# Whole-row activation loads, zero matmuls in idle gaps, output stores ahead of the branch, a fourth split-weight pair and a fourteenth expert buffer in a hybrid RG-LRU, Conformer and expert trunk

## The chip, the cores and the metric

The kernel runs on one core of a Trainium2 chip. The metric is the device time of one execution in microseconds (us). Three runs of the kernel before gave 1893.31, 1895.31 and 1895.43 us; the median is 1895.31 us.

## What is computed

Two layers of a diffusion trunk over 256 latent tokens and 256 context tokens, 1024 channels wide, in float32. Both streams share the weights.

```python
for i in range(DEPTH):                       # DEPTH = 2
    mod = split(silu(c) @ mod_w[i] + mod_b[i], 6)           # shifts, scales, gates; also from c_ctx
    h = modulate(rmsnorm(x, norm1_g[i]), mod[0], mod[1])
    # mixer: one input projection, two branches, merged by gates
    u_rnn, g_rnn, u_glu, g_glu, g_mrg = split(h @ w_in[i])
    hf, hb = rglru_bidir(u_rnn, ...)         # conv of width 4, gates, one scan per direction
    y_a = ((hf + hb) * gelu(g_rnn)) @ w_a
    y_b = silu(layernorm(dwconv31(u_glu * sigmoid(g_glu)))) @ w_b
    x = x + mod[2] * ((g_a * y_a + g_b * y_b) @ w_out)
    h = modulate(rmsnorm(x, norm2_g[i]), mod[3], mod[4])
    # layer 0: SwiGLU of width 2816; layer 1: top 2 of 8 SwiGLU experts of width 2816
    x = x + mod[5] * ffn(h)
return rmsnorm(x, final_g)                   # the 256 latent tokens alone
```

The latent scans start from the final state of the context scans. In layer 1 the context is only needed for that state.

## The kernel before

**Layout and precision.** Channels lie on the 128 partitions, in 8 blocks (index k), tokens along the row. `X[k]` holds a block's context tokens (`xc`, 256 columns) and latent tokens (`xs`, 256 columns). A float32 weight or activation is split into a high and a low half by `split` and `hilo`: ScalarE rounds the high half (`wh`, `nh`, line 153), VectorE subtracts it from the whole for the low half (`wl`, `nl`, line 154). A product is then three matmuls: high by high, low by high, high by low (lines 273 to 275; in the first projection lines 418 to 420).

**Weights.** Two streams, both issued by SyncE. The dense one, `raw`, comes in chunks of 2 MB with two buffers; a chunk is four pieces of 128x1024, and a piece is one block of 128 output channels of a projection, with 24 matmuls on a split piece. The split pieces live in the pool `hl`, with three pairs `wh`, `wl` before the change. The expert stream, `mraw`, comes in 264 transfers of 1 MB, in two rings of 9 and 4 buffers (`RINGA`, `RINGB`).

**Start.** SyncE issues the small vector constants, `sc` (from which silu(c) is made), the first modulation chunk `m0`, and x in eight transfers of 256 KB. TensorE multiplies the modulation (`pmod`, line 369, and its transposition `pmt`, line 379), then sums squares over channels (`colsum`: `pcol`, line 284; `rstd_cols`: `pst`, line 308, a square root on ScalarE and a reciprocal on VectorE), and spreads the result over the partitions (`spread`: `dg`, line 320, `prs`, line 322). `norm` makes `nt`, `nh` and `nl` from it, and the projection `pu` begins.

**Order of work.** A tile scheduler places the instructions of all engines by priorities and dependencies, so a larger pool moves instructions on engines that the diff does not name. In the mixers TensorE works through the projection while VectorE does convolutions (`cv`), the blocks of recurrent scans (lines 546 to 558) and the low halves `wl`, all in one queue.

**Experts.** `route` and `route_sort` choose two experts per token (`sel`, `pos`, the one-hot `oh`), sort the experts by load, and gather their tokens (`pgat`, `xe`). Every expert is 11 chunks. A chunk is an up projection (`up_big`, lines 1191 to 1193, eight blocks by three matmuls), a swish (`hd`, line 1212), a transposition of the result (`turn_big`: `pht`, line 1219, then the split `hh`, `hlo`) and a down projection (`down_big`, lines 1250 to 1252). The loop in `experts` is staggered: the up projection of chunk n+1 stands ahead of the down projection of chunk n, and `pht` of chunk n right behind its own up projection. Four experts of the eight take up to 128 tokens each ("big"), four take up to 64 ("small"); big and small alternate.

**End.** After the last expert the squares of the latent tokens are summed again, `rsf` is taken, and then every engine branches on whether some expert had too many tokens (line 1111). The body behind the branch repeats the experts for the rest and does not run with these inputs. Behind it stand `spread`, eight multiplications of 128x256 on VectorE (line 1119) and eight stores of 128 KB (line 1120).

Of the kernel before, what the change touches and what calls it, by code (L numbers as in the profile page):

```python
# [6 lines left out]
F32 = mybir.dt.float32  # L7
# [34 lines left out]
RINGA, RINGB, XB = 9, 4, 1  # L42
# [89 lines left out]
class Trunk:  # L132
    def __init__(self, ctx, tc, wd, wm, wv, sr, xt, vec, out, dbg=None, stop=None):
        self.tc, self.nc = tc, tc.nc
        self.wv, self.sr = wv, sr
        self.wd, self.wm, self.xt_d, self.vec_d, self.out = wd, wm, xt, vec, out
        self.dbg, self.stop = dbg or {}, stop
        self.ci = DEPTH
        self.ahead = 100
        self.last_act = None  # L140
        self.gate = None
# [137 lines left out]
    def colsum(self, get, n, tag):  # L279
        nc = self.nc  # L280
        ps = self.ps("pcol")
        for k in range(KD):
            g = k % 4
            nc.tensor.matmul(ps[32 * g:32 * g + 32, 0:n], self.v("om", 0, 32), get(k), start=(k < 4), stop=(k >= 4),
                             tile_position=(0, 32 * g))
        ev = self.t2(tag, "cev")
        nc.scalar.copy(ev[:, 0:n], ps[:, 0:n])
        return ev
# [13 lines left out]

    def rstd_cols(self, ev, n, rs=None):
# [3 lines left out]
        for t in range(nt):  # L307
            nc.tensor.matmul(pt[:, 2 * t:2 * t + 2], ev[:, t * P:(t + 1) * P], self.v("s32", 0, 2), start=True,
                             stop=True)
# [6 lines left out]
    def spread(self, rs, n, tag):  # L316
        nc = self.nc
        dg = self.t2(tag, "dg")
        for t in range(n // P):
            nc.vector.tensor_scalar(dg[:, t * P:(t + 1) * P], self.v("id", 0, P), rs[:, t:t + 1], None, op0=ALU.mult)  # L320
        r = self.ps("prs")
        nc.tensor.matmul(r[:, 0:n], self.v("o1", 0, P), dg[:, 0:n], start=True, stop=True)  # L322
# [35 lines left out]
    def mod_chunk(self, i, q, pool=None, got=None):  # L358
# [7 lines left out]
        for kk in range(2):  # L366
            for g in range(4):
                k = 2 * g + kk
                nc.tensor.matmul(ps[32 * g:32 * g + 32, :], self.sc[:, k, 6 - 2 * r:38 - 2 * r], w[:, k, :],
                                 start=(r == 0 and kk == 0), stop=(end and kk == 1), tile_position=(0, 32 * g))  # L370
# [7 lines left out]
        for t in range(4):  # L378
            nc.tensor.matmul(pt[:, n * t:n * t + n], ev[:, t * P:(t + 1) * P], self.v("sel", 0, n), start=True,
                             stop=True)  # L380
# [22 lines left out]
    def begin(self, X, hx, m0):  # L403
# [409 lines left out]
    def run(self, ctx):  # L813
# [17 lines left out]
        self.hl = left.enter_context(tc.tile_pool(name="hl", bufs=3))  # L831
# [6 lines left out]
        self.start = start.__enter__()  # L838
        m0 = self.chunk(("mod", 0, 0), self.start)
# [138 lines left out]
    def route_end(self):  # L978
# [3 lines left out]
        rs = self.rstd_cols(ev, TC)  # L982
        rt_t = lambda nm, shape: mp.tile(shape, F32, tag=nm, name=nm)
# [24 lines left out]
        nc.tensor.matmul(pv[:, 1, :], tri, sel[:, 1, :], start=False, stop=True)  # L1008
# [87 lines left out]
    def moe(self, X):  # L1096
# [6 lines left out]
        rs = self.mp.tile([P, 4], F32, tag="rsf", name="rsf")  # L1103
# [202 lines left out]
    def experts(self, X, xe):  # L1306
# [4 lines left out]
        for n in range(len(steps) + 2):  # L1311
# [36 lines left out]
            prev = (*new[:2], (self.turn_big if new[0] < BIG else self.turn_small)(new[2])) if new else None  # L1348
# [110 lines left out]
```

## Time and profile before

| | us |
|---|---|
| median of three runs | 1895.31 |
| the profiled execution | 1895.52 |
| its span on the core | 1893.6 |
| TensorE matmuls busy (PE) | 1835.2 |
| VectorE busy (DVE) | 1299.9 |
| ScalarE busy (ACT) | 893.7 |
| data moved | 449.64 MB, mean 237 GB/s |

The span is what the trace covers; the profiled execution took 1.9 us more than it. PE is TensorE's matmuls, PEld its weight loads, DVE VectorE, ACT ScalarE, POOL GpSimd, SP SyncE; a q behind a name is the engine's instruction queue. A row of the timeline gives the start, the duration, the engine, the source line, the operation, what it writes and reads, how many alike follow one another, and in brackets how long the engine stood idle before it and what it waited for.

### The profile page before, as it was taken

What the parts mean: (1) busy time and instruction counts of PE and PEld (TensorE: products, weight loads), DVE (VectorE), ACT (ScalarE), POOL (GpSimd) and SP (SyncE); (2) the same over time, 40 slices, a digit from 0 to 9 for tenths busy, and PEclk for the clock granted to TensorE, in tenths of its full rate; (3) what the DMA queues carried; (4) which work ended last, traced back from release to release, by engine and by line L of the source; (5) the groups of instructions that cost most, each with busy time, mean ns of one, the idle gap of its engine ahead of it and who ended that gap; (6) DMA issues with size and microseconds to landing.
All of it is one profiled execution on the core that took longest, in us unless ns stands there. A gap on an engine that the chain in (4) does not pass through costs nothing. (4 is left out here: it accounts for less than half of the span.)

```text
span 1893.6 us, 26822 instructions
## 1 busy us (share of the span) xinstructions
PE 1835.2 (97%) x10292; PEld 1421.2 (75%) x10292; DVE 1299.9 (69%) x2296; ACT 893.7 (47%) x1266; POOL 0.4 (0%) x5
## 2 busy tenths in 40 slices
PE   6999999999999999999998999999999999999997
PEld 3666777778998888888787998787577568667853
DVE  3899996255679967656999565885298249518922
ACT  4695332253552222225797554674176137416711
POOL 0000000000000000000000000000000000000000
PEclk9999999999999999999999999899999999999998
DMA  8233444222335565421243447689999999999994
GB/s 346 106 112 139 178 178 178 89 89 89 112 116 200 182 225 190 156 89 46 106 151 134 166 180 308 256 339 376 419 420 405 396 420 420 383 413 420 415 386 166
DMA packets 66951, 449.64 MB, mean 237 GB/s; under 512 B 7424, under 2 KB 8576, under 8 KB 24704
## 3 DMA queue, kind: packets, MB, share of 16 engines
q1 hardware_dynamic: 66816, 447.85, 60.5%
q8 instruction: 83, 1.36, 0.3%
q14 instruction: 52, 0.43, 0.1%
HBM read 446.78 MB, written 1.05 MB: 236 GB/s over the span
## 5 line engine op out<-in xcount | busy, mean ns | idle before, releaser
L153 ACT ACTIVATE wh<-raw 128x1024 fp32r<-128x1024 f32 (+1 forms) x237 | 247.3, 1053 | 500.5 <-PE ps L274 317.0
L154 DVE TENSOR_TENSOR wl<-raw,wh 128x1024 fp32r<-128x1024 f32 (+1 forms) x237 | 286.6, 1218 | 137.7 <-ACT wh L153 134.4
L154 DVE TENSOR_TENSOR wl<-mraw,wh 128x1024 fp32r<-128x1024 f32 x264 | 314.6, 1222 | 35.8 <-ACT wh L153 29.2
L153 ACT ACTIVATE wh<-mraw 128x1024 fp32r<-128x1024 f32 x264 | 272.8, 1057 | 51.6 <-PE s L1192 37.6
L273 PE MATMUL ps<-nh,wh 128*128 128x512 f32 (+1 forms) x736 | 273.1, 371 | 1.0 <-ACT wh L153 1.0
L275 PE MATMUL ps<-nh,wl 128*128 128x512 f32 (+1 forms) x736 | 269.5, 366 | 3.1 <-DVE wl L154 3.1
L274 PE MATMUL ps<-nl,wh 128*128 128x512 f32 (+1 forms) x736 | 269.2, 366 | 0.0
L273 PEld LDWEIGHTS ps<-nh,wh 128*128 128x128 f32 x736 | 139.2, 189 | 31.1 <-ACT gab L256 1.7
L1203 PE MATMUL s<-mraw,xes 128*64 128x256 f32 x1408 | 161.9, 380 | 0.0
L275 PEld LDWEIGHTS ps<-nh,wl 128*128 128x128 f32 x736 | 139.0, 189 | 27.7 <-DVE wl L154 3.3
L274 PEld LDWEIGHTS ps<-nl,wh 128*128 128x128 f32 x736 | 139.1, 189 | 25.3 <-issue 1.4
L1193 PE MATMUL s<-wl,xe 128*128 128x512 f32 x352 | 140.6, 399 | 4.2 <-DVE wl L154 4.2
L256 ACT ACTIVATE hd<-s 128x256 f32<-128x256 f32 (+1 forms) x88 | 28.9, 329 | 242.6 <-PE s L1203 218.6
L1191 PE MATMUL s<-wh,xe 128*128 128x512 f32 x352 | 143.0, 406 | 0.0
L1192 PE MATMUL s<-wh,xe 128*128 128x512 f32 x352 | 138.8, 394 | 0.0
L1203 PEld LDWEIGHTS s<-mraw,xes 128*64 128x64 f32 x1408 | 98.2, 137 | 45.0 <-issue 0.7
L1212 DVE TENSOR_TENSOR hd<-hd,s 128x256 f32<-128x256 f32 (+1 forms) x88 | 31.0, 352 | 129.9 <-ACT hd L256 129.8
L572 DVE SCALAR_TENSOR_TENSOR cv<-v,vec,cv 128x254 f32<-128x254 f32 (+14 forms) x240 | 103.6, 481 | 0.8
L232 DVE SCALAR_TENSOR_TENSOR junk<-wv,scr 128x512 f32<-128x512 f32 x128 | 84.1, 687 | 0.2
L1193 PEld LDWEIGHTS s<-wl,xe 128*128 128x128 f32 x352 | 66.9, 190 | 23.0 <-DVE wl L154 8.9
L1258 PE MATMUL y<-mraw,hs 128*64 128x512 f32 x352 | 83.4, 594 | 0.4 <-DVE hs L1237 0.4
L1191 PEld LDWEIGHTS s<-wh,xe 128*128 128x128 f32 x352 | 67.2, 191 | 13.4 <-ACT wh L153 0.7
(283 smaller groups left out, 3540.2 us busy)
## 6 DMA issues: line engine op xcount, KB each, us to landing
mraw<-in_wm_dram SPq DMA_DIRECT2D x264, 1024.0 KB, 9.5
raw<-in_wd_dram SPq DMA_DIRECT2D x65, 2048.0 KB, 7.4
wv<-in_wv_dram SPq DMA_DIRECT2D x96, 256.0 KB, 3.6
lw<-in_wd_dram SPq DMA_DIRECT2D x16, 256.0 KB, 2.9
xc<-in_xt_dram SPq DMA_DIRECT2D x4, 256.0 KB, 10.2
xs<-in_xt_dram SPq DMA_DIRECT2D x4, 256.0 KB, 10.3
scr<-in_sr_dram SPq DMA_DIRECT2D x4, 256.0 KB, 4.9
out_dram<-xs SPq DMA_DIRECT2D x8, 128.0 KB, 2.0
```

The costliest lines, as they stand in the source:

```text
L153: return (self.nc.scalar.activation(hi, src, AF.Copy), self.nc.vector.tensor_tensor(lo, src, hi.bitcast(F32), op=ALU.subtract))
L154: self.nc.vector.tensor_tensor(lo, src, hi.bitcast(F32), op=ALU.subtract))
L232: nc.vector.scalar_tensor_tensor(junk, w[h], 1.0, rows[2 * s + h], op0=ALU.mult, op1=ALU.mult, accum_out=acc[:, h, s:s + 1])
L273: self.nc.tensor.matmul(o, wh, ah, start=(k == 0), stop=False)
L274: self.nc.tensor.matmul(o, wh, al, start=False, stop=False)
L275: self.nc.tensor.matmul(o, wl, ah, start=False, stop=(k == KD - 1))
L572: nc.vector.scalar_tensor_tensor(cv[:, a0:a1], v[:, a0 + d:a1 + d], w(t), cv[:, a0:a1], op0=ALU.mult, op1=ALU.add)
L1191: nc.tensor.matmul(p1, xe[0][:, k, :], wh[:, cs], start=(k == 0), stop=False)
L1192: nc.tensor.matmul(p1, xe[1][:, k, :], wh[:, cs], start=False, stop=False)
L1193: nc.tensor.matmul(p1, xe[0][:, k, :], wl[:, cs], start=False, stop=(k == KD - 1))
L1203: nc.tensor.matmul(p1[r, 0:2 * P].rearrange("p (g f) -> p g f", g=2), xe[:, k, :], w[:, :, h * P:(h + 1) * P], start=(k == 0), stop=(k == ...
L1258: ins = self.nc.tensor.matmul(py[0][r, :], hs[:, f * HALF:(f + 1) * HALF], raw[:, f * PIECE + q * 512:f * PIECE + (q + 1) * 512], start=(c ...
```

## The change

1. **Start.** x comes in two transfers of 1 MB, `xs` second in SyncE's order and `xc` fourth, ahead of `m0`. The squares are shared between ScalarE and VectorE (`square2`). The sums of squares and `spread` stand ahead of the first modulation, which now follows `prs`. The first weight chunk comes in two halves. `dg` is one instruction in place of one per 128 columns. The square root's table is loaded early.
2. **Zero matmuls.** `warm(n)` issues n matmuls on a zero tile whose result nobody reads, ordered behind the last real matmul: 3 of 512 columns ahead of `pcol`, single ones and a pair of 256 columns between the steps of the start, 6 behind `pst` and 4 behind `ppos` in the routing.
3. **Pools.** `hl` has four pairs in place of three; `RINGB` is 5 in place of 4; the DMA scratch of the program is 1 KB.
4. **Experts.** The transposition of the first chunk (n = 0) is put off until after the up projection of the second.
5. **End.** The scale by the final norm's weight (`fg`), `spread`, four multiplications of 128x512 and four stores of 256 KB stand ahead of the branch, and again in its body. Behind the branch nothing is left.

```diff
-RINGA, RINGB, XB = 9, 4, 1
+RINGA, RINGB, XB = 9, 5, 1
...
+    def warm(self, n, cols=TC):
+        ps = self.ps("pwarm")
+        for _ in range(n):
+            ins = self.nc.tensor.matmul(ps[:, 0:cols], self.wz[:, 0:P], self.wz[:, 0:cols], start=True, stop=True).ins
+            if self.last_pe is not None:
+                self.order(ins, self.last_pe)
...
+    def square2(self, tiles):
+        def get(k):
+            sq = self.t2("g", "sq")
+            for s in range(2):
+                x, o = tiles[k][s], sq[:, s * TC:(s + 1) * TC]
+                if (k + s) % 2:
+                    self.nc.vector.tensor_tensor(o, x, x, op=ALU.mult)
+                else:
+                    self.nc.scalar.activation(o, x, AF.Square)
+            return sq
...
-        for t in range(n // P):
-            nc.vector.tensor_scalar(dg[:, t * P:(t + 1) * P], self.v("id", 0, P), rs[:, t:t + 1], None, op0=ALU.mult)
+        nt = n // P
+        nc.vector.tensor_tensor(dg[:, 0:n].rearrange("p (t m) -> p t m", t=nt),
+                                self.v("id", 0, P).unsqueeze(1).to_broadcast([P, nt, P]),
+                                rs[:, 0:nt].unsqueeze(2).to_broadcast([P, nt, P]), op=ALU.mult)
...
-        for _ in self.mod_chunk(0, 0, got=m0):
-            pass
-        ev = self.colsum(self.square(X, 0, T, "g"), T, "g")
-        r = self.spread(self.rstd_cols(ev, T), T, "g")
-        raw = self.chunk(tuple(what))
+        self.warm(3, 512)
+        ev = self.colsum(self.square2(X), T, "g")
+        self.warm(1)
+        rs = self.rstd_cols(ev, T)
+        self.warm(1)
+        r = self.spread(rs, T, "g")
+        m = self.mod_chunk(0, 0, got=m0)
+        next(m)
+        self.warm(1)
+        next(m, None)
+        self.warm(2)
+        self.last_pe, self.wz = None, self.vec[:, VO["id"]:VO["id"] + 512]
+        raw = self.chunk(tuple(what), parts=2)
...
+        nc.sync.dma_start(self.sc, self.vec_d[:, NV:NV + KD * SCW].rearrange("p (k m) -> p k m", m=SCW))
+        nc.sync.dma_start(xs, self.xt_d[1])
         nc.sync.dma_start(self.vec[:, 0:NV0], self.vec_d[:, 0:NV0])
...
+        nc.sync.dma_start(xc, self.xt_d[0])
         m0 = self.chunk(("mod", 0, 0), self.start)
-        for k in range(0, KD, 2):
-            for s, t in enumerate((xc, xs)):
-                nc.sync.dma_start(t[:, k:k + 2, :], self.xt_d[s, :, k:k + 2, :])
...
-        self.hl = left.enter_context(tc.tile_pool(name="hl", bufs=3))
+        self.hl = left.enter_context(tc.tile_pool(name="hl", bufs=4))
...
         rs = self.rstd_cols(ev, TC)
+        self.warm(6)
...
+        self.last_pe = nc.tensor.matmul(pv[:, 1, :], tri, sel[:, 1, :], start=False, stop=True).ins.name
+        self.warm(4)
...
             self.experts(X, xe)
-            self.rstd_cols(self.colsum(self.square(X, TC, T, "rt"), TC, "rt"), TC, rs)
+            rs = self.rstd_cols(self.colsum(self.square(X, TC, T, "rt"), TC, "rt"), TC)
+            o = [self.mp.tile([P, 4, TC], F32, tag=nm, name="o") for nm in ("yl", "yh")]
+            for k in range(KD):
+                nc.vector.tensor_scalar(o[k // 4][:, k % 4], X[k][1], self.v("fg", k), None, op0=ALU.mult)
+            r = self.spread(rs, TC, "rt")
+            for k in range(0, KD, 2):
+                t = o[k // 4][:, k % 4:k % 4 + 2]
+                nc.vector.tensor_tensor(t, t, r[:, 0:TC].unsqueeze(1).to_broadcast([P, 2, TC]), op=ALU.mult)
+                nc.sync.dma_start(self.out[:, k:k + 2, :], t)
...
-        r = self.spread(rs, TC, "rt")
-        for k in range(KD):
-            nc.vector.scalar_tensor_tensor(X[k][1], X[k][1], self.v("fg", k), r[:, 0:TC], op0=ALU.mult, op1=ALU.mult)
-            nc.sync.dma_start(self.out[:, k, :], X[k][1])
...
+                if n == 1:
+                    ph = self.turn_big(ph)
                 big = pe < BIG
...
+            prev = new if n == 0 else (*new[:2], (self.turn_big if new[0] < BIG else self.turn_small)(new[2])) if new else None
...
+    nc = _bacc.Bacc("TRN2", target_bir_lowering=False, num_devices=1, dynamic_dma_scratch_size=1024)
```

In the changed file the lines of the expert loop stand 38 further down (1191 becomes 1229), those of the scans 32 further (546 becomes 578). Three places of the order are shown.

TensorE's first instructions, before the change: the modulation first, then the sums of squares and the projection.

```order
L369 MATMUL pmod<-raw,sc 32x512 x8
L379 MATMUL pmt<-vec,ev 128x2 x4
L284 MATMUL pcol<-sq,vec 32x512 x8
L308 MATMUL pst<-vec,cev 128x2 x4
L322 MATMUL prs<-dg,vec 128x512
L418 MATMUL pu<-nh,wh 128x512
```

The same place after the change (`pwarm` are the zero matmuls):

```order
L272 MATMUL pwarm<-wz 128x512 x3
L292 MATMUL pcol<-sq,vec 32x512 x8
L272 MATMUL pwarm<-wz 128x256
L329 MATMUL pst<-vec,cev 128x2 x4
L272 MATMUL pwarm<-wz 128x256
L345 MATMUL prs<-dg,vec 128x512
L392 MATMUL pmod<-raw,sc 32x512 x8
L272 MATMUL pwarm<-wz 128x256
L403 MATMUL pmt<-vec,ev 128x2 x4
L272 MATMUL pwarm<-wz 128x256 x2
L442 MATMUL pu<-nh,wh 128x512
```

The modulation went from the head to behind `prs`, and every gap between dependent steps holds zero matmuls.

VectorE in the first layer's mixer, before the change, in one of the blocks of scans (`gi`, `r`, `hs` are its tiles; the listing gives a scan the name of its family, the trace calls it a scan; `wl` is the low half of a weight piece, `v` the gated input of the Conformer branch):

```order
L552 SCALAR_TENSOR_TENSOR r<-a,r,gi 128x256
L548 SCALAR_TENSOR_TENSOR r<-a,gi 128x512
L546 TENSOR_TENSOR gi<-gi,e_1254 128x512
L558 TENSOR_TENSOR hs<-r 128x512
L550 SCALAR_TENSOR_TENSOR r<-a,gi 128x256
L154 TENSOR_TENSOR wl<-raw,wh 128x1024
L552 SCALAR_TENSOR_TENSOR r<-a,r,gi 128x256
L154 TENSOR_TENSOR wl<-raw,wh 128x1024
L558 TENSOR_TENSOR hs<-r 128x512
```

The same block after the change, from its fourth operation:

```order
L582 SCALAR_TENSOR_TENSOR r<-a,gi 128x256
L578 TENSOR_TENSOR gi<-gi,e_1257 128x512
L584 SCALAR_TENSOR_TENSOR r<-a,r,gi 128x256
L580 SCALAR_TENSOR_TENSOR r<-a,gi 128x512
L578 TENSOR_TENSOR gi<-gi,e_1263 128x512
L590 TENSOR_TENSOR hs<-r 128x512
L582 SCALAR_TENSOR_TENSOR r<-a,gi 128x256
L155 TENSOR_TENSOR wl<-raw,wh 128x1024
L584 SCALAR_TENSOR_TENSOR r<-a,r,gi 128x256
L688 SCALAR_TENSOR_TENSOR v<-v,pglu 128x512
L590 TENSOR_TENSOR hs<-r 128x512
```

The first of the two `wl` has left the block and stands ten rows ahead of its first scan operation; the second stands where the first stood.

TensorE at the first experts' chunks, before the change (`s_10522` is the up projection of chunk 0, `s_10573` that of chunk 1):

```order
L1191 MATMUL s_10522<-wh,xe_10422 128x512
L1192 MATMUL s_10522<-wh,xe_10423 128x512
L1193 MATMUL s_10522<-wl,xe_10422 128x512
L1219 MATMUL pht<-vec,hd 128x128 x2
L1191 MATMUL s_10573<-wh,xe_10422 128x512
L1192 MATMUL s_10573<-wh,xe_10423 128x512
```

After the change (`s_10578` is the up projection of chunk 1, `y` the down projection of chunk 0):

```order
L1229 MATMUL s_10578<-wh,xe_10435 128x512
L1230 MATMUL s_10578<-wh,xe_10436 128x512
L1257 MATMUL pht<-vec,hd 128x128 x2
L1231 MATMUL s_10578<-wl,xe_10435 128x512
L1229 MATMUL s_10578<-wh,xe_10435 128x512
L1230 MATMUL s_10578<-wh,xe_10436 128x512
L1231 MATMUL s_10578<-wl,xe_10435 128x512
L1288 MATMUL y<-wh,hh 128x512
```

The transposition of chunk 0 moved from ahead of chunk 1's 24 matmuls to ahead of the last four of them.

## Rows read from the trace of the kernel before

**Rows 1.** The page's head: span, and busy time of each engine.

```profile
span 1893.6 us, 26822 instructions
PE 1835.2 (97%) x10292; PEld 1421.2 (75%) x10292; DVE 1299.9 (69%) x2296; ACT 893.7 (47%) x1266; POOL 0.4 (0%) x5
```

**Rows 2.** Stretches of the span: busy time by engine, granted clock, DMA share, GB/s.

```profile
0.00:20.00 20.00, 7.28 (x36) 2.99 (x40) 0.33 (x2) 7.45 (x19) 0.38 (x5) 1.00 0.90 328
...
80.00:150.00 70.00, 70.00 (x277) 47.77 (x276) 68.31 (x109) 61.45 (x84) 0.00 (x0) 1.00 0.31 113
...
1177.00:1870.00 693.00, 676.82 (x3943) 482.19 (x3942) 419.37 (x599) 338.85 (x468) 0.00 (x0) 0.99 0.96 387
...
1340.00:1400.00 60.00, 58.61 (x355) 38.14 (x352) 31.76 (x45) 25.25 (x34) 0.00 (x0) 1.00 1.01 420
```

**Rows 3.** Timeline of the start, 10 to 38 us.

```profile
11.93 3.64 PE L369 MATMUL pmod<-raw,sc 128*32 128x512 f32 x16 [11.93 <-DMA raw<-in_wd_dram]
...
17.48 0.72 ACT L298 ACTIVATE sq<-xs 128x256 f32<-128x256 f32 x2
...
18.15 3.64 PE L284 MATMUL pcol<-sq,vec 128*32 128x512 f32 x16
...
18.46 0.16 DVE L398 SCALAR_TENSOR_TENSOR gs<-mod,vec 128x4 f32<-128x4 f32 x1
...
28.04 0.48 DVE L349 SCALAR_TENSOR_TENSOR nt<-xc,gs,prs 128x256 f32<-128x256 f32 x1 [2.17 <-PE prs L322]
...
32.27 0.63 PE L420 MATMUL pu<-nh,wl 128*128 128x512 f32 x1
...
36.11 0.63 PE L420 MATMUL pu<-nh,wl 128*128 128x512 f32 x1
```

**Rows 4.** Timeline of the first layer's mixer, 178 to 184 us.

```profile
178.42 1.21 DVE L154 TENSOR_TENSOR wl<-raw,wh 128x1024 fp32r<-128x1024 f32 x1
...
179.68 0.50 PE L275 MATMUL pglu<-nh,wl 128*128 128x512 f32 x1 [1.83 <-DVE wl L154]
...
180.71 0.62 PE L273 MATMUL pglu<-nh,wh 128*128 128x512 f32 x1
...
183.68 0.60 PE L274 MATMUL pglu<-nl,wh 128*128 128x512 f32 x1
```

**Rows 5.** Timeline from the routing to the first down projection.

```profile
1196.51 1.23 DVE L154 TENSOR_TENSOR wl<-mraw,wh 128x1024 fp32r<-128x1024 f32 x1 [0.65 <-ACT wh L153]
...
1204.02 0.44 PE L1219 MATMUL pht<-vec,hd 128*128 128x128 f32 x2 [3.07 <-DVE hd L1212]
...
1211.34 0.39 PE L1250 MATMUL y<-wh,hh 128*128 128x512 f32 x1
```

**Rows 6.** Timeline of the end.

```profile
1881.10 0.17 DVE L313 RECIPROCAL rsf<-rsf 128x2 f32<-128x2 f32 x1 [3.62 <-ACT rsf L256]
1885.07 0.48 DVE L320 TENSOR_SCALAR dg<-vec,rsf 128x128 f32<-128x128 f32 x2 [3.80 <-DVEq L1111]
1885.70 1.19 PE L322 MATMUL prs<-dg,vec 128*128 128x256 f32 x2 [4.93 <-DVE dg L320]
1886.93 3.22 DVE L1119 SCALAR_TENSOR_TENSOR xs<-xs,vec,prs 128x256 f32<-128x256 f32 x8 [1.38 <-PE prs L322]
1887.44 3.77 SPq L1120 DMA_DIRECT2D out_dram<-xs  x8
```

**Rows 7.** Line 1111, the branch, by queue: duration in ns, first and last start.

```profile
L1111 SPq EVENT_SEMAPHORE  x8: 17/17/17, 1853.7 to 1864.4; - x8
...
L1111 SPq COMPARE_BRANCH  x1: 53/53/53, 1848.6 to 1848.6; - x1
...
L1111 DVEq EVENT_SEMAPHORE  x1: 21/21/21, 1884.9 to 1884.9; - x1
```

**Rows 8.** DMA issues of the whole run: count, KB each, median us to landing.

```profile
out_dram<-xs SPq DMA_DIRECT2D x8, 128.0 KB, 2.0
```

**Rows 9.** Waits of SyncE's queue in the whole run: us in total, times, longest.

```profile
SPq L920 <- DVE wl L154: 220.9, 78, 12.4
```

More of the change, by code (lines that the diff above doesn't have):

```diff
@@ L140, in __init__ @@
         self.last_act = None
+        self.last_pe = None
         self.gate = None
@@ L283, in colsum @@
             g = k % 4
-            nc.tensor.matmul(ps[32 * g:32 * g + 32, 0:n], self.v("om", 0, 32), get(k), start=(k < 4), stop=(k >= 4),
-                             tile_position=(0, 32 * g))
+            self.last_pe = nc.tensor.matmul(ps[32 * g:32 * g + 32, 0:n], self.v("om", 0, 32), get(k), start=(k < 4),
+                                            stop=(k >= 4), tile_position=(0, 32 * g)).ins.name
         ev = self.t2(tag, "cev")
@@ L301, in square @@
         return get
+    def square2(self, tiles):
[8 more added lines that the diff above has]
+            return sq
+        return get
     def rstd_cols(self, ev, n, rs=None):
@@ L307, in rstd_cols @@
         for t in range(nt):
-            nc.tensor.matmul(pt[:, 2 * t:2 * t + 2], ev[:, t * P:(t + 1) * P], self.v("s32", 0, 2), start=True,
-                             stop=True)
+            self.last_pe = nc.tensor.matmul(pt[:, 2 * t:2 * t + 2], ev[:, t * P:(t + 1) * P], self.v("s32", 0, 2),
+                                            start=True, stop=True).ins.name
         rs = self.small.tile([P, 4], F32, tag="rs", name="rs") if rs is None else rs
@@ L318, in spread @@
         dg = self.t2(tag, "dg")
-        for t in range(n // P):
-            nc.vector.tensor_scalar(dg[:, t * P:(t + 1) * P], self.v("id", 0, P), rs[:, t:t + 1], None, op0=ALU.mult)
+        nt = n // P
+        nc.vector.tensor_tensor(dg[:, 0:n].rearrange("p (t m) -> p t m", t=nt),
+                                self.v("id", 0, P).unsqueeze(1).to_broadcast([P, nt, P]),
+                                rs[:, 0:nt].unsqueeze(2).to_broadcast([P, nt, P]), op=ALU.mult)
         r = self.ps("prs")
-        nc.tensor.matmul(r[:, 0:n], self.v("o1", 0, P), dg[:, 0:n], start=True, stop=True)
+        self.last_pe = nc.tensor.matmul(r[:, 0:n], self.v("o1", 0, P), dg[:, 0:n], start=True, stop=True).ins.name
         return r
@@ L368, in mod_chunk @@
                 k = 2 * g + kk
-                nc.tensor.matmul(ps[32 * g:32 * g + 32, :], self.sc[:, k, 6 - 2 * r:38 - 2 * r], w[:, k, :],
-                                 start=(r == 0 and kk == 0), stop=(end and kk == 1), tile_position=(0, 32 * g))
+                self.last_pe = nc.tensor.matmul(ps[32 * g:32 * g + 32, :], self.sc[:, k, 6 - 2 * r:38 - 2 * r],
+                                                w[:, k, :], start=(r == 0 and kk == 0), stop=(end and kk == 1),
+                                                tile_position=(0, 32 * g)).ins.name
         if not end:
@@ L378, in mod_chunk @@
         for t in range(4):
-            nc.tensor.matmul(pt[:, n * t:n * t + n], ev[:, t * P:(t + 1) * P], self.v("sel", 0, n), start=True,
-                             stop=True)
+            self.last_pe = nc.tensor.matmul(pt[:, n * t:n * t + n], ev[:, t * P:(t + 1) * P], self.v("sel", 0, n),
+                                            start=True, stop=True).ins.name
         if single:
@@ L821, in run @@
         nc.gpsimd.memset(self.mod[1], 0.0)
+        nc.sync.dma_start(self.sc, self.vec_d[:, NV:NV + KD * SCW].rearrange("p (k m) -> p k m", m=SCW))
+        nc.sync.dma_start(xs, self.xt_d[1])
         nc.sync.dma_start(self.vec[:, 0:NV0], self.vec_d[:, 0:NV0])
-        nc.sync.dma_start(self.sc, self.vec_d[:, NV:NV + KD * SCW].rearrange("p (k m) -> p k m", m=SCW))
         self.act_f(self.sc, self.sc, AF.Silu)
+        self.preload(AF.Sqrt)
         W = dict(reuse_waits="tile")
@@ L838, in run @@
         self.start = start.__enter__()
+        self.wz = self.t2("g", "wz")
+        nc.gpsimd.memset(self.wz, 0.0)
+        nc.sync.dma_start(xc, self.xt_d[0])
         m0 = self.chunk(("mod", 0, 0), self.start)
-        for k in range(0, KD, 2):
-            for s, t in enumerate((xc, xs)):
-                nc.sync.dma_start(t[:, k:k + 2, :], self.xt_d[s, :, k:k + 2, :])
         hx = self.pairs("hx")
@@ L1007, in route_end @@
         nc.tensor.matmul(pv[:, 1, :], one, sel[:, 0, :], start=True, stop=False)
-        nc.tensor.matmul(pv[:, 1, :], tri, sel[:, 1, :], start=False, stop=True)
+        self.last_pe = nc.tensor.matmul(pv[:, 1, :], tri, sel[:, 1, :], start=False, stop=True).ins.name
+        self.warm(4)
         self.tok, t = [], []
@@ L1347, in experts @@
                     tail = None
-            prev = (*new[:2], (self.turn_big if new[0] < BIG else self.turn_small)(new[2])) if new else None
+            prev = new if n == 0 else (*new[:2], (self.turn_big if new[0] < BIG else self.turn_small)(new[2])) if new else None
         while tail:
@@ L1446 @@
     from concourse.bass_utils import run_bass_kernel_spmd as _run
-    nc = _bacc.Bacc("TRN2", target_bir_lowering=False, num_devices=1)
+    nc = _bacc.Bacc("TRN2", target_bir_lowering=False, num_devices=1, dynamic_dma_scratch_size=1024)
     arrays, args = {}, []
```

1 line of the change is left out of this document (removed).

## The prediction

> **What bounds the kernel now.** I read the head of the page first. TensorE's matmuls fill 1835.2 of 1893.6 us, VectorE 1299.9, ScalarE 893.7 [rows 1]. So the end can only move by what TensorE spends idle, 58.4 us with the gaps between modelled ends, or by what it runs at the lower of its two clock levels (1.2 and 2.4 GHz). The stretches show where that is. In the first 20 us TensorE is busy for 7.28 us while the DMA engines are 0.90 busy; from 80 to 150 us it is never idle, and VectorE is busy for 68.31 of the 70 us; in the expert part, 1177 to 1870 us, it is idle for 16.2 of 693 us, and the DMA engines are at 0.96 [rows 2]. Next come the timelines of the places that the change touches. At the start, TensorE waits 11.93 us for the modulation's weights, and the first normalized tile `nt` is made at 28.04 [rows 3]. In the mixer it waits once for 1.83 us for a low half `wl` that VectorE began behind scans [rows 4]. At the first experts' chunks it waits 3.07 us for `hd` [rows 5]. At the end it waits 4.93 us for `dg`, and VectorE waits for its own branch for 3.80 of them [rows 6]. The span of the profiled execution is 1893.6 and its time 1895.52, so 1.9 us lie around it; that time is 0.2 above the median of 1895.31.
>
> **Start.** The chain to `nt` is now x, squares, `pcol`, `pst`, `prs`, and `pcol` stands behind the modulation on TensorE. After the change, 1 MB of `xs`, the constants and 1 MB of `xc` come ahead of the 2 MB of `m0`. At the 328 GB/s of the first 20 us [rows 2], these 2.5 MB take 7.6 us; with some 2 us until the first bytes move (my estimate), `xc` lands between 9.6 us and the 11.93 at which about as many bytes had brought `m0` [rows 3]; I take 10.8. Two squares take 0.72 us [rows 3], so eight on each of two engines take 2.9 and hide behind `pcol`'s own 3.64: `pcol` begins at 11.3 and ends at 14.9, where it ended at 21.79. From there to `nt` the trace needs 6.2 us (28.04); the single `dg` and two zero matmuls about balance: 21.1. But the modulation now stands behind `prs`: 3.64 for `pmod`, and from its end (15.57) to that of `gs` (18.62) another 3.05. `nt` then begins at 27.8, against 28.04 [rows 3]. So it is if the clock stays at its low level: a gain of 0.2. If the denser work has raised the clock by the time of `prs`, TensorE's share of the steps behind it is halved, `nt` comes at 25.0, and the first matmuls of `pu`, 0.43 us apart over the nine steps from 32.27 to 36.11 [rows 3], stand half as far apart, 2.4 us for the first twelve: together 5.4. With all of it at full clock it is 8.7. Before, TensorE was busy with small gaps from 11.93 to 21.79, and the matmuls still took 0.63 us at 32 to 36 (the clock column of that stretch says 1.00 [rows 2]; I go by the spacing, which is twice that of full clock); so I take 4.0, between the case that only `pu` profits (2.6) and the 5.4. Bounds: 0 and 8.7. The zero matmuls lie in gaps; where one is late it costs 0.2 to 0.4 us.
>
> **Fourth pair.** In the mixer the order shows what it does: the `wl` for which TensorE waits 1.83 us [rows 4] moves ahead of the block of scans. The wait is gone. The next `wl` takes the place of the first, some 0.8 us later than before (one `wl` of 1.21 more ahead of it, one convolution step less); a piece feeds 24 matmuls, over 5 us at either clock, so it has that long until it is needed. What goes with the wait is the low clock behind it: from 180.71 to 183.68 a matmul takes 0.6 us and more as at the start [rows 3, 4], for some 3.4 us, half of which, 1.7, is lost. That is 3.5 in all. Where else is a split moved? Ahead of other scan blocks, where TensorE doesn't wait now; there `hs` comes up to 1.2 us later, and from 80 to 150 us VectorE has only 1.7 us to spare [rows 2]. I take 3.0, bounds 0 and 3.5. Waits for a `wl` in the second layer keep their neighbours in the changed order.
>
> **Routing and first experts.** Now: up projection 0 ends at 1200.95, 3.07 us ahead of the `pht` at 1204.02, which waits for `hd`; ScalarE loads a table for it; VectorE's next `wl` but one comes late, since ScalarE stands with `wh` behind TensorE; the clock falls; the first down projection begins at 1211.34 [rows 5]. After the change TensorE goes straight on to the up projection 1, and VectorE's queue is `wl` 3 to 6, `hd`, `wl` 7 and 8, `hlo`. VectorE then sets the pace: from the `wl` 3 at 1196.51 on, five `wl` at 1.23, 0.29 and 0.28 for the sorted weights and 0.42 for `hd` end at 1203.65, and some four matmuls later, 0.9 us, the down projection can begin: 1204.5. The zero matmuls in the routing can bring `wl` 3 forward by its idle 0.65 [rows 5]: 1203.9. I take 1204.1, a gain of 7.2. Bounds: 6.0, if the new transposition costs a wait of 1.2 in its turn, and 8.5, if `wl` 3 comes 1.3 earlier still because the whole gather runs at the high clock.
>
> **End.** The branch now lies behind the stores. `rs` is ready at 1881.06 as before; the reciprocal ends at 1881.27; `dg` at once rather than at 1885.07, `prs` at 1881.8 for 1.19; four multiplications of 512 columns at the 0.6 us pitch of the scans' 128x512 operations instead of eight that take 3.22 [rows 6]: VectorE is done at 1885.5. The eight scalings by `fg` lie in VectorE's idle 3.62 us ahead of the reciprocal [rows 6], at 0.39 each. The last store is issued at 1885.6 and lands after 2.0 [rows 8] to 3 us, 1888.6 at the latest. Behind it stand the branches. VectorE's takes, with its register's load, from 1881.27 to 1884.9 and `dg` at 1885.07; SyncE's took 5.1 us, 1848.6 to 1853.7, while its queue loaded weights [rows 7]. So VectorE is through at 1889.3, SyncE, after 3.1 to 5.1, between 1889.1 and 1891.1. I allow 0.9 us from the last engine to the end of the span (1893.6 now, with the last store issued at 1891.21 and landed 2.0 later at the most often): 1890.2 to 1892.0. I take 1890.4, since SyncE's queue is nearly empty by then, a gain of 3.2; bounds 1.6 and 3.6.
>
> VectorE stands still for 3.80 us at the branch [rows 6]. The Trainium skill, "Runtime: NRT & Kernel Launch", "Instruction fetch mechanics", says that a taken branch outside of the prefetched window waits for a fetch of its target page; the trace agrees with its 3.80. By that rule the branch costs as much behind the stores as ahead of them, and only the work that it held up is gained. If the branch were hidden there, the stores would set the end, and it would be 1889.5 by the row of the stores [rows 8], 0.9 us earlier than by that rule.
>
> **Buffers and scratch.** None of TensorE's waits in the trace is for `mraw`. A transfer of 1 MB takes 2.5 us where the stream is full, at 420 GB/s [rows 2]; 264 of them take 660 of the 693 us, and a pair of a big and a small expert has 173 us for its 66 transfers of 165. SyncE waits for buffers to come free, 220.9 us for the splits alone [rows 9], so the stream follows the engines and not they the stream. The fourteenth buffer gives 2.5 us more lead where none is short: 0, bounds 0 and 0.5. All loads go by SyncE's queue, so the scratch is space alone: 0.
>
> **Sum.** 4.0 + 3.0 + 7.2 + 3.2 = 17.4: span 1876.2, time 1878.1 against 1895.52, against the median 1878.0.
>
> **Rivals.** (a) The start's clock stays low, SyncE's branch takes 5.1 us at the end, and half of the mixer's gain is lost to later `hs`: 0.2 + 1.5 + 7.2 + 1.6 = 10.5, that is 1884.9. For it: the clock did not rise before 36 us; against it: the gaps are filled now. (b) The clock is high from the squares on, and every term is at its better end: 8.7 + 3.5 + 8.5 + 3.6 = 24.3, 1871.0; half-way to it 1874.5. (c) No change: the expert stream is the bound. It is at 0.96 of 693 us [rows 2], and if its 33 idle us lie ahead of the first chunk, while the rings are full, it ends when it ended, and only the end's 3.2 remain: 1892.1. For it: the share; against it: the waits for free buffers [rows 9], which come earlier with the engines. (d) Slower: the splits moved ahead of scans. The two mixers have eight scan blocks, and VectorE is full around them [rows 2]. If every block made TensorE wait as one does now, 1.83 us and 1.7 of low clock [rows 4], that is 28 us in place of the 3.5: -17.4 + 3.0 + 28 = +13.6, 1908.9. It decides from six blocks on. Against it: `hs` is 1.2 us later at most, and nothing reads it until the rest of the projection is done.
>
> **Chances.** The sum's own case, 1875 to 1882: 0.52. (a), 1882 to 1889: 0.20. (b), below 1875: 0.16. (c), 1891.5 to 1899: 0.06; (d), above: 0.04; the last 0.02 lie between 1889 and 1891.5. The range 1872 to 1887 leaves out (c), (d) and what lies between, 0.12, and 0.08 of the tails of (a) and (b). This measurement can tell about 0.2%, 3.8 us. Faster by more than that: 0.90; within: 0.06; slower: 0.04.
>
> **What would show it.** Start: `xc` landing at 10 to 11 us, `nt` at 24 to 27.5, the matmuls of `pu` 0.21 to 0.23 apart; wrong if `nt` comes after 28. Mixer: no wait at `pglu` near 174 and no stretch of 0.63 us matmuls behind it; wrong if other `wl` or `hs` waits stand there. Experts: the first down projection 7 us earlier against the routing's `sel`, no wait of 3 us; wrong if VectorE's `wl` 7 comes later than seven operations behind `wl` 3. End: `dg` right behind the reciprocal, branches as the last rows, 9.3 us from the reciprocal to the end of the span. The forecast fails most easily by the start's clock and by waits in the mixers that no order shows.

## The result and the profile after

The changed kernel takes 1872.11 us (median of four runs, 1871.77 to 1873.71) where the kernel before took 1895.26 beside it: a ratio of 0.9888, 95% interval 0.9876 to 0.9900. That is 23.2 us less; forecast were 17.3 less, 1878.0, within 1872 to 1887, so the time lies 0.11 us inside the range, and one of the four executions outside of it. The profiled execution took 1872.05 with a span of 1870.3.

The page's head of the changed kernel answers to [rows 1]:

```profile
span 1870.3 us, 26861 instructions
PE 1831.2 (98%) x10328; PEld 1420.8 (76%) x10328; DVE 1300.2 (70%) x2296; ACT 889.9 (48%) x1259; POOL 0.8 (0%) x6
```

Stretches of the changed kernel, for [rows 2] (the second is the mixer of [rows 4], the last the expert part, begun 20 us earlier):

```profile
0.00:20.00 20.00, 13.58 (x44) 5.66 (x48) 3.73 (x10) 6.64 (x14) 0.85 (x6) 0.78 0.92 375
160.00:200.00 40.00, 38.34 (x173) 29.43 (x172) 39.66 (x82) 12.31 (x16) 0.00 (x0) 1.00 0.43 158
1157.00:1849.00 692.00, 682.03 (x4021) 488.29 (x4019) 419.90 (x601) 339.57 (x470) 0.00 (x0) 1.00 0.96 387
```

The busy times are nearly those of before; TensorE's idle time went from 58.4 to 39.1 us. To see where, I laid the starts of the same matmuls in both traces side by side. The lead of the changed kernel grows in six places:

| stretch, in the time of before | lead grows by, us | forecast |
|---|---|---|
| start, until the second `pmod` (36.67, now 32.44) | 4.2 | 4.0 |
| rest of the first layer, until 860 | 3.3 | 3.0 |
| second layer, until `sel` of the routing (1181.94, now 1169.27) | 5.2 | 0 |
| routing and first experts, until the first down projection (1211.34, now 1192.22) | 6.4 | 7.2 |
| experts, until `rs` at the end (1880.80, now 1859.63) | 2.1 | 0 |
| the end (1893.6, now 1870.3) | 2.2 | 3.2 |

Two terms that the forecast did not have, 7.3 us, make up more than its 6 us too little. The start of the changed kernel, beside [rows 3]:

```profile
9.47 0.42 ACT L319 ACTIVATE sq<-xc 128x256 f32<-128x256 f32 x1 [2.29 <-DMA xc<-in_xt_dram]
...
9.94 4.54 PE L292 MATMUL pcol<-sq,vec 128*32 128x512 f32 x16 [4.24 <-DVE sq L317]
...
19.05 3.07 PE L392 MATMUL pmod<-raw,sc 128*32 128x512 f32 x16
...
24.32 0.48 DVE L372 SCALAR_TENSOR_TENSOR nt<-xc,gs,prs 128x256 f32<-128x256 f32 x1
24.72 1.22 DVE L155 TENSOR_TENSOR wl<-raw,wh 128x1024 fp32r<-128x1024 f32 x1
...
27.32 0.49 PE L442 MATMUL pu<-nh,wh 128*128 128x512 f32 x1 [2.46 <-ACT nh L375]
...
30.38 0.63 PE L442 MATMUL pu<-nh,wh 128*128 128x512 f32 x1
...
31.66 0.39 PE L442 MATMUL pu<-nh,wh 128*128 128x512 f32 x1
```

`xc` is there at 9.47, `nt` comes at 24.32, 3.7 us earlier; a `wl` of 1.22 us then stands between it and the next step, `pu` waits 2.46, the clock falls behind that wait, and the matmuls take 0.63 us again until 31.2. The three zero matmuls ahead of `pcol` do not reach it: `pcol` stands behind 4.24 us of idle time.

The routing and the first experts of the changed kernel, beside [rows 5]:

```profile
1183.14 1.23 DVE L155 TENSOR_TENSOR wl<-mraw,wh 128x1024 fp32r<-128x1024 f32 x1 [0.42 <-ACT wh L154]
...
1190.72 0.38 PE L1257 MATMUL pht<-vec,hd 128*128 128x128 f32 x2
...
1192.22 0.40 PE L1288 MATMUL y<-wh,hh 128*128 128x512 f32 x1
```

No wait stands ahead of `pht`. From `wl` 3 to the first down projection it is 9.1 us, where it was 14.8. From 1175 to 1193 us TensorE has one wait, of 0.4 for the gather at the start of this stretch. It is ScalarE's `wh`, and behind them VectorE's `wl`, that wait for TensorE (`s` is the up projection):

```profile
PE pgat L1193 <- DVE tkl L1065: 0.4, 1, 0.4
```

```profile
1183.49 1.06 ACT L154 ACTIVATE wh<-mraw 128x1024 fp32r<-128x1024 f32 x1 [0.38 <-PE s L1230]
```

The end of the changed kernel, beside [rows 6]:

```profile
1859.92 0.17 DVE L334 RECIPROCAL rs<-rs 128x2 f32<-128x2 f32 x1 [1.53 <-ACT rs L257]
1860.19 0.42 DVE L341 TENSOR_TENSOR dg<-vec,rs 128x256 f32<-128x256 f32 x1
...
1860.67 0.75 PE L345 MATMUL prs<-dg,vec 128*128 128x256 f32 x2 [1.08 <-DVE dg L341]
1861.46 2.48 DVE L1148 TENSOR_TENSOR o<-o,prs 128x512 f32<-128x512 f32 x4 [0.84 <-PE prs L345]
1862.17 2.52 SPq L1149 DMA_DIRECT2D out_dram<-o  x4
```

Its branch line (queue, duration in ns, first and last start), beside [rows 7]:

```profile
L1153 SPq EVENT_SEMAPHORE  x8: 17/17/17, 1868.4 to 1868.9; - x8
...
L1153 DVEq COMPARE_BRANCH  x1: 72/72/72, 1862.1 to 1862.1; - x1
...
L1153 SPq COMPARE_BRANCH  x1: 53/53/53, 1864.7 to 1864.7; - x1
...
L1153 DVEq EVENT_SEMAPHORE  x1: 21/21/21, 1865.4 to 1865.4; - x1
```

`dg` follows the reciprocal at once. VectorE's branch begins at 1862.1, while its multiplications still run, and is through at 1865.4. SyncE's begins behind its last store, takes 3.7 us and is through last.

### The profile page after: what moved, and what is told of

It reads as the page before. It is cut to its first block, busy times and chain, and to the rows that moved or that the text cites. A ratio compares the mean times of both kernels' runs of the same rounds, so it can differ in the third digit from the quotient of the medians.

```text
span 1870.3 us, 26861 instructions
## 1 busy us (share of the span) xinstructions
PE 1831.2 (98%) x10328; PEld 1420.8 (76%) x10328; DVE 1300.2 (70%) x2296; ACT 889.9 (48%) x1259; POOL 0.8 (0%) x6
## 4 chain that ended last, share of the span: by engine, by line
PE 86%; DVE 10%; ACT 2%; DMA 1%; issue 1%; SPq 0%; ACTq 0%; DVEq 0%
PE ps L281 11%; PE ps L283 11%; PE ps L282 11%; PE s L1241 8%; PE s L1231 4%; PE y L1296 4%; PE s L1229 4%; PE s L1230 4%; DVE wl L155 2%; PE y L1290 2%; PE y L1288 2%; PE y L1289 2%; PE ps L780 2%; PE ps L779 2%; PE ps L781 2%; PE pcol L292 1%
## 5 line engine op out<-in xcount | busy, mean ns | idle before, releaser
L604 DVE SCALAR_TENSOR_TENSOR cv<-v,vec,cv 128x251 f32<-128x251 f32 (+14 forms) x240 | 102.4, 469 | 0.7
L1231 PEld LDWEIGHTS s<-wl,xe 128*128 128x128 f32 x352 | 66.4, 189 | 23.2 <-DVE wl L155 9.2
```

What stands on the lines that cost most here:

```text
L604: nc.vector.scalar_tensor_tensor(cv[:, a0:a1], v[:, a0 + d:a1 + d], w(t), cv[:, a0:a1], op0=ALU.mult, op1=ALU.add)
L1231: nc.tensor.matmul(p1, xe[0][:, k, :], wl[:, cs], start=False, stop=(k == KD - 1))
```

## Experiments

Most undo or add one thing in the changed kernel. Ratios are to the kernel before, run beside it; spans, of single profiled executions, are compared with 1870.3. The kernel before took 1889.88 to 1897.11 us in its single executions beside these runs. The intervals of three pairs, the old end, the default scratch and both kernels with five pairs lie clear of the changed kernel's; those of the seven others overlap it, and what is said of these rests on single traces.

**No zero matmuls** (`warm` returns at once).

> The changed kernel without any zero matmul; all else stays. Theory 1 (they raise the clock where it pays): the steps of the start behind the sums of squares run at the low level again. In the changed kernel pst took 1.05 us, pmt 1.05, pmod 3.07 and prs 1.62, against 1.87, 1.87, 3.64 and 2.08 before, so the first nt comes some 2.7 us later (27.0 for 24.3), the low level lasts longer into pu, another 1 us, and the routing loses 0.5 to 1: 4 to 5 us in all, a time near 1876.5. Theory 2 (the real matmuls, closer together now, raise it alone): within 1 us of the changed kernel, 1872 to 1873, with matmuls 0.43 us apart in no stretch where they were not before.

1873.01 us, 0.9898 (0.9881 to 0.9914), span 1871.2. Theory 2 by the time, with a split that neither had: up to the routing this kernel is 0.8 to 0.9 us *ahead* of the changed one, from there to the first down projection it loses 2.0. So those of the routing (there they multiply the constants `vec`, not zeros) are worth 2. The clock shows it, first the changed kernel, then this one:

```profile
1180.00:1185.00 5.00, 5.00 (x19) 4.02 (x18) 4.09 (x18) 3.91 (x6) 0.00 (x0) 0.81 0.37 157
```

```profile
1180.00:1185.00 5.00, 5.00 (x14) 3.89 (x13) 2.88 (x12) 3.09 (x4) 0.00 (x0) 0.54 0.22 92
```

Of those at the start no gain shows. But the start can't resolve so little: the second `pmod`, at 32.44 us in the changed kernel and at 31.98 here, comes at 30.60 to 32.65 in five kernels below (transposition, thirteen buffers, old end, sixteen bytes, ScalarE's queue) whose start is that of the changed one.

**Three pairs.**

```diff
-        self.hl = left.enter_context(tc.tile_pool(name="hl", bufs=4))
+        self.hl = left.enter_context(tc.tile_pool(name="hl", bufs=3))
```

> The changed kernel with three split-weight pairs instead of four. Theory 1 (the fourth pair is worth more than the prediction's 3.0, because it also lets the splits of the second layer's first part run ahead): the wait of 1.8 us near 174 and the low clock behind it come back, 3.4 us, and the 4.5 us that the changed kernel gained between 866 and 1008 us are lost too: 7 to 8 us, a time near 1880. Theory 2 (the gain in the second layer comes from elsewhere): only the 3.4 us come back, 1875.5.

1879.31, 0.9935 (0.9917 to 0.9952), span 1876.1, 5.8 more. Of it 5.0 us arise between 860 and 1010, as theory 1 had it. But in the first layer only 1.6 us arise, and this execution had begun 1.7 ahead. With three pairs TensorE waits 1.97 us at the place of [rows 4], and its clock does not fall; with four it still waits 1.12 and 0.5. In the mixer, three pairs, and the granted clock (last but two) of the stretch, first before the change, then with three pairs:

```profile
173.77 0.51 PE L283 MATMUL pglu<-nh,wl 128*128 128x512 f32 x1 [1.97 <-DVE wl L155]
```

```profile
160.00:200.00 40.00, 38.17 (x166) 28.34 (x165) 40.00 (x81) 18.86 (x24) 0.00 (x0) 0.96 0.43 158
```

```profile
160.00:200.00 40.00, 38.03 (x170) 29.24 (x171) 40.00 (x81) 16.30 (x21) 0.00 (x0) 1.00 0.50 179
```

Another part of the first layer is a modulation chunk. Its 16 matmuls stood apart before the change, 10 and 6, and do with three pairs; with four they stand together:

```profile
142.77 1.90 PE L369 MATMUL pmod<-raw,sc 128*32 128x512 f32 x10
...
164.96 1.06 PE L369 MATMUL pmod<-raw,sc 128*32 128x512 f32 x6
```

```profile
138.49 1.93 PE L392 MATMUL pmod<-raw,sc 128*32 128x512 f32 x16
```

Sixteen take no longer than ten. By the starts of the matmuls behind them the split costs 1.1 to 1.2 us.

The second layer shows one thing that the pair does. This is the kernel with three pairs, where the squares of the latent tokens are summed for the second layer's norm:

```profile
887.25 0.62 PE L292 MATMUL pcol<-sq,vec 128*32 128x256 f32 x2
887.29 1.06 ACT L154 ACTIVATE wh<-raw 128x1024 fp32r<-128x1024 f32 x1 [2.84 <-PE pu L282]
888.26 1.01 ACT L306 ACTIVATE sq<-xs 128x256 f32<-128x256 f32 x3
...
888.71 1.23 PE L292 MATMUL pcol<-sq,vec 128*32 128x256 f32 x6 [0.85 <-ACT sq L306]
```

ScalarE stands 2.84 us with a `wh` for which no pair is free until TensorE is through with one, and the last three squares stand behind it in the queue. TensorE, which has to free the pair, then waits for the squares. It was so before the change (first row below). With four pairs the same `wh` comes behind the last square:

```profile
894.76 1.06 ACT L153 ACTIVATE wh<-raw 128x1024 fp32r<-128x1024 f32 x1 [2.83 <-PE pu L274]
```

```profile
880.79 2.12 ACT L306 ACTIVATE sq<-xs 128x256 f32<-128x256 f32 x5
...
885.88 1.06 ACT L154 ACTIVATE wh<-raw 128x1024 fp32r<-128x1024 f32 x1 [2.96 <-PE pu L282]
```

This place is 1.7 of the 5.0 us. 1.3 come earlier, in the sums of the context's squares: ScalarE works in the same order there and TensorE never waits, but `pcol` stands in three groups among the `pdn` with three pairs and in one with four:

```profile
858.57 0.62 PE L292 MATMUL pcol<-sq,vec 128*32 128x256 f32 x2
...
859.79 0.64 PE L292 MATMUL pcol<-sq,vec 128*32 128x256 f32 x8
...
862.35 0.63 PE L292 MATMUL pcol<-sq,vec 128*32 128x256 f32 x6
```

```profile
860.49 1.07 PE L292 MATMUL pcol<-sq,vec 128*32 128x256 f32 x16
```

1.0 is a wait at 1000.8 for `v`, which stands behind a `wh` on ScalarE with three pairs and not with four; the last 1.0 lies spread between.

**Transposition in its old place** (the two lines of the loop in `experts` as before).

> The changed kernel with the first chunk's transposition back behind its own up projection. Theory 1 (the transposition's place is the gain at the first experts): the wait of 3 us for hd and the low clock behind it come back, first down projection 5.5 to 7 us later, a time near 1878.5. Theory 2 (VectorE, ahead by the zero matmuls in the routing, sets the pace in either order): 1 to 3 us, 1874.

1875.79, 0.9909 (0.9892 to 0.9927), span 1874.4. The wait of 3.07 is back, and the down projection comes 4.6 us later:

```profile
1189.55 0.69 PE L1257 MATMUL pht<-vec,hd 128*128 128x128 f32 x2 [3.07 <-DVE hd L1250]
...
1196.86 0.39 PE L1288 MATMUL y<-wh,hh 128*128 128x512 f32 x1
```

This lies between the theories: 4.5 for the place, 2.0 for the zero matmuls, together about the 6.4 of the table.

**Thirteen expert buffers** (`RINGB` 4).

> The changed kernel with 13 expert buffers instead of 14. Theory 1 (the stream follows the engines and has lead): no change, 1872 within 1 us. Theory 2 (the 1.4 us that the changed kernel gained between 1208 and 1800 us come from the buffer): 1873.5, with the loss spread over the four pairs of experts.

1871.47, 0.9887 (0.9870 to 0.9904), span 1870.3, the matmuls within 0.4 us but for a moment in the first mixer: theory 1.

**x in pieces of 256 KB, at the new places.**

```diff
-        nc.sync.dma_start(xs, self.xt_d[1])
+        for k in range(0, KD, 2):
+            nc.sync.dma_start(xs[:, k:k + 2, :], self.xt_d[1, :, k:k + 2, :])
```

(`xc` likewise.)

> The changed kernel with xs and xc loaded in four pieces of 256 KB each, at the places in SyncE's order where the changed kernel loads them whole. Theory 1 (what counts is that x comes ahead of the modulation's weights, not the size of a transfer): xc complete within 0.5 us of the changed kernel's 9.47, the first nt within 0.7 us of 24.3, 1872 to 1873. Theory 2 (whole rows save issue time and semaphore waits): the last pieces wait as before, when one was issued at 11.81 only; xc complete 2 us or more later, nt with it, 1874 or more.

1874.46, 0.9896 (0.9879 to 0.9912), span 1871.5. The first square of `xc` begins 0.9 us later (10.37), `nt` comes at 24.83, and from 40 us on 0.3 us are left, 0.0 at the last matmuls of the experts; the span's difference lies at the end, where SyncE's branch begins 0.4 later and takes 4.3 us in this execution. By the median this is theory 2's range; by the trace the size of a transfer is worth 0.3 us at most, as theory 1 had it. That x comes first was not undone in any run.

**Modulation ahead of the sums of squares, x still first** (the calls of `mod_chunk` in front of `colsum`).

> The changed kernel with the modulation's matmuls ahead of the sums of squares on TensorE, as before, and x still loaded first. Theory 1 (the start's gain of 4 to 5 us is that the sums of squares no longer wait behind the modulation): pcol begins behind m0's landing and pmt, near 17 us and not at 9.9, and nt near 25.5 to 27 instead of 24.3, up to 3 us lost, near 1874.5. Theory 2 (the sum of both is the same chain in either order, 3.1 + 3.1 us of matmuls; only the loads matter): within 1 us.

1873.54, 0.9895 (0.9877 to 0.9913), span 1870.8. `nt` comes at 26.46, as theory 1 had it, but `pu` follows it with shorter waits: from 180 us on this kernel is 0.9 to 1.0 us ahead, until the wait for a `wl` at 1018 us, in the second layer, takes it back. By the spans, 0.5 apart, this is theory 2, though not by its reason; the medians, 1.4 apart, lie between the two.

**The old end.**

> The changed kernel with the end of the kernel before: the branch ahead of the eight multiplications and the eight stores. Theory 1 (the branch costs the same wherever it stands; what it held up, dg to the last store, is what moves): from the reciprocal to the end of the span 12.5 us as before instead of 10.4, 2.1 to 2.3 us lost, near 1874.3. Theory 2 (the branch behind the stores is mostly hidden by their landing): 3.2 us or more lost, 1875.3 and above.

1879.46, 0.9923 (0.9906 to 0.9939), span 1877.3, 7.0 more: in theory 2's range, but not by its reason. At the branch VectorE stood 6.06 us, not the 3.80 of [rows 6]. The branch itself took 3.1 of them, from its compare to its next event, where it had taken 3.2 (1881.7 to 1884.9):

```profile
1862.20 0.17 DVE L334 RECIPROCAL rsf<-rsf 128x2 f32<-128x2 f32 x1 [3.62 <-ACT rsf L257]
1868.43 0.43 DVE L341 TENSOR_TENSOR dg<-vec,rsf 128x256 f32<-128x256 f32 x1 [6.06 <-issue]
```

```profile
L1147 DVEq COMPARE_BRANCH  x1: 72/72/72, 1862.8 to 1862.8; - x1
...
L1147 DVEq EVENT_SEMAPHORE  x1: 21/21/21, 1865.9 to 1865.9; - x1
```

The end is 4.7 us longer. 2.4 of it lie behind the branch, where VectorE waits for nothing that the profile shows; the 2.3 that are left are what theory 1 said. The other 2.3 of the 7.0 came earlier, at about 0.07 us a chunk in the down projections of the big experts: the fifth line of the table, undone by a change that touches none of their instructions. (This kernel has the tile `rsf` again.)

**Default scratch, three pairs, thirteen buffers.**

> The changed kernel with three pairs, 13 expert buffers and the default DMA scratch, to be read against the one with three pairs alone (1879.3, span 1876.1). Theory 1 (the 2 us that the changed kernel gains in steps of 0.13 us in the down projections of the big experts from 1380 us on come from where the tiles lie in the scratch-freed memory): the steps go, the span is 2 us longer, 1878. Theory 2 (the scratch and the buffer are space alone): 1876.1 within 0.5, the same steps.

1879.49, 0.9923 (0.9907 to 0.9940), span 1877.4. Against three pairs alone the start is 1.5 us later, with the same instructions in the same order, and nothing is added in the experts: theory 2 for them.

**Sixteen bytes.**

```diff
+        pad = self.mp.tile([P, 4], F32, tag="rsf", name="rsf")
+        nc.vector.memset(pad, 0.0)
```

> The changed kernel with one more tile of 16 bytes per partition (zeroed once, never read) in the experts' pool, at the place where the kernel before had rsf, and nothing else. Theory 1 (the 2 us that come and go in steps of 0.13 us in the big experts' down projections depend on where the tiles behind rsf lie): the steps come back between 1380 and 1800 us, 2.1 us more at 1800, span 1872.4, and the down projection's matmuls stand 0.234 us apart instead of 0.227. Theory 2 (the steps belong to the order of the end): no steps, 1870.3.

1875.01, 0.9891 (0.9875 to 0.9908), span 1873.7. From 1180 to the end of the experts it loses 2.3 us in the same steps: theory 1, by the trace. In every undisturbed chunk these matmuls start 0.233 us apart in the three kernels with a tile at that place (before, old end, this one) and 0.227 in the eleven others. The three lines of the big experts' down projection, 1210 to 1850 us, with the mean ns of one; first the changed kernel, then the one with the pad:

```profile
L1288 PE MATMUL y<-wh,hh 128*128 128x512 f32 x168 | 66.1, 393 | 4.0 <-ACT wh L154 4.0
L1289 PE MATMUL y<-wh,hlo 128*128 128x512 f32 x168 | 65.5, 390 | 0.0
L1290 PE MATMUL y<-wl,hh 128*128 128x512 f32 x168 | 58.9, 394 | 0.2
```

```profile
L1291 PE MATMUL y<-wh,hh 128*128 128x512 f32 x168 | 66.9, 398 | 4.0 <-ACT wh L154 4.0
L1292 PE MATMUL y<-wh,hlo 128*128 128x512 f32 x168 | 66.2, 394 | 0.0
L1293 PE MATMUL y<-wl,hh 128*128 128x512 f32 x168 | 59.9, 400 | 0.2
```

**Stores from ScalarE's queue** (`nc.scalar.dma_start`).

> The changed kernel with the four stores issued by ScalarE's queue instead of SyncE's. Theory 1 (SyncE's branch behind its last store is the last link: 1864.7 to 1868.4 of a span that ends at 1870.3): SyncE branches as soon as it has loaded its register, ScalarE's branch (2.4 us from its compare to its event in the changed kernel) stands behind the stores, and the end comes 0.8 to 1.5 us earlier: span 1868.8 to 1869.5. Theory 2 (VectorE's branch, from 1863.9, or the landing of the last store is as late): within 0.4 us.

1871.28, 0.9878 (0.9862 to 0.9895), span 1868.7. SyncE branched at 1824, but ScalarE's branch, now behind the stores, took 3.5 us (1864.2 to 1867.7). From `rs` to the end it is 10.4 us against 10.7: theory 2. The rest of the span's difference arose at the start.

**Five pairs.**

```diff
-        self.hl = left.enter_context(tc.tile_pool(name="hl", bufs=4))
+        self.hl = left.enter_context(tc.tile_pool(name="hl", bufs=5))
```

> The changed kernel with a fifth split-weight pair. Theory 1 (each pair lets the low halves stand further ahead of the scan blocks): the wait of 3.1 us at 1018 us shrinks and the second layer's first part gains again, 2 to 4 us, a time near 1869. Theory 2 (VectorE is full from 900 to 1030 us, so a piece can only be split earlier at the cost of something that is waited for as well): within 1 us of the changed kernel, with waits in other places.

1863.88, 0.9834 (0.9817 to 0.9850): theory 1 and more, 8 us below the changed kernel by the medians. The profiled execution was the slowest of the four (1868.35; the others 1862.60 to 1864.63), so the trace shows only 3.7 of the 8. No wait is left near 177, the lead grows by 4.6 us between 860 and 1030, and the wait of 3.1 there is 2.3:

```profile
PE ps L283 <- DVE wl L155: 2.3, 1, 2.3
```

**Five pairs, zero matmuls in the routing alone.**

> Five split-weight pairs, and the zero matmuls in the routing alone, none at the start; all else as changed. Theory 1 (the zero matmuls of the start do nothing for the time, as the kernel without any was 0.5 to 0.9 us ahead until the routing; the ones in the routing are worth 2): 1863 to 1864, no slower than five pairs with all zero matmuls (1863.9). Theory 2 (with five pairs the start's splits run further ahead, and a clock that is up early is worth something): 1865 to 1867.

1866.03 (1863.49 to 1866.49), 0.9850 (0.9834 to 0.9866). The median lies in theory 2's range, but the interval overlaps that of five pairs with all zero matmuls; which of the two is faster stays open. Five pairs, with either, beat both kernels.

## Why the forecast held, and where it did not

The number held by little, and in part by luck: two terms that I had at 0 gave 7.3 us, and two that I had too high took 1.8 back. The sum's own case, 1875 to 1882, did not come.

**Start: near in size, the mechanism not shown.** I put the 4.0 between clock levels that denser work would raise. The clock did rise twice (granted 1.00 from 16 to 18 us and from 22 to 28) and fell again (0.50 from 18 to 20, 0.56 from 28 to 30); without any zero matmul the start was no later. Zero matmuls, whole rows (0.3 us) and the place of the modulation are each worth less than the 2 us by which kernels with the same start differ. What is left, and common to all these kernels, is x ahead of the modulation's weights, with the shared squares and the halved first chunk. None of these was undone, so which of them gives the 4.2 stays open.

**Fourth pair: the step that failed is "waits for a `wl` in the second layer keep their neighbours".** True of the `wl`, and the 3.1 us wait did stay. But I looked for the pair's worth only where TensorE waits for a `wl`, and put the second layer at 0. Taking the pair away costs 5.0 us there. ScalarE's queue, where a `wh` stands ahead of squares and of `v`, is 2.7 of them; 1.3 are the order of `pcol` on TensorE, 1.0 is not explained. In the first layer 3.3 came for 3.0, but otherwise than I said. 1.2 is the modulation chunk that no longer stands apart. 1.5 is the low clock that is gone, near the 1.7 that I had, but it was no part of the pair and its coming was luck: of the 14 kernels profiled, the granted clock of 160 to 200 us is 0.96 in two, the kernel before and the one with the pad, which has four pairs, and 1.00 in the one with the longest wait. The wait shrank from 1.83 to 1.12 and 0.5 only; it is gone with five pairs, and also with four where the modulation stands ahead.

**Routing and experts: near in size, but VectorE does not set the pace.** 6.4 of 7.2 came. I had VectorE's queue take 8.0 us from `wl` 3 to the first down projection; it was 9.1, with TensorE never waiting in it. The wait of 3.07 went, as said, and the up projections ran at a higher clock (granted 0.69 from 1205 to 1210 us before, 1.00 from 1185 to 1195 now). The zero matmuls let `wl` 3 come 0.7 us earlier (0.65 said) and gave 2.0 in all by the kernel without them, more than I allowed them; the transposition gave 4.5.

**End: mis-sized, 2.2 for 3.2.** VectorE was through 5.5 us behind the reciprocal rather than 8.2, since its branch ran beside its multiplications. SyncE's branch began behind its last store's issue, at 1864.7, took 3.7, and 1.9 us followed it where I allowed 0.9; this allowance is what was too small. The rule that I took from the Trainium skill, "Runtime: NRT & Kernel Launch", "Instruction fetch mechanics", is that a taken branch whose target lies outside of the prefetched window waits for a fetch of the target's page. These rows agree with it in that the branch takes 3.3 to 4.4 us on SyncE and 3.5 on ScalarE behind the stores, and 3.0 to 3.3 on VectorE; that it is a fetch they do not show. The old end in the new program lost 2.4 us more behind VectorE's branch, and why stays open. Against that end the new one is worth 4.7.

**Not foreseen: 2.1 us in the experts**, because the tile `rsf` went. Of the rivals, the start's clock did stay low in parts, as in (a), and the time came out most of the way to (b)'s 1871.0, but not by (b)'s cause. Neither (c) nor (d) showed: the expert stream kept its 0.96 and followed TensorE by 20 us, and of the scans' `hs` no wait arose.

## What to carry to other kernels

Here a pool of split tiles that was one pair short cost more where its consumer's waits for it did not change than at the wait for which the pair was added. Look in the producer's queue for an instruction that waits for a free buffer, and at what stands behind it, and undo a pool's size alone. Zero matmuls gave 2.0 us here in a chain with two up projections without a wait behind it, and nothing that could be measured between waits; measure them by leaving them out. When an edit seems to move time in a part that it does not touch, test the place of the tiles with a pad before looking for a cause in the order.

## What was not expected of the hardware

One more tile of 16 bytes per partition in the experts' pool changed a 128x512 matmul's mean duration from 393 to 398 ns, in the down projections of the big experts, 2.1 to 2.3 us in all. Which tile's place it is was not tried. VectorE stood 3.80 us and 6.06 us at the same branch in two programs, though the branch itself took 3.2 and 3.1. And the granted clock fell behind a wait of 1.83 us in one program and not behind one of 1.97 in another.
